# A two-layer conv and pooling trunk: the two-chunk FFN part starts at tile 6 instead of 8, a down group moves ahead of layer 1, and the second chunk's pooling mixer goes to VectorE in two halves

## Chip, core and metric

The kernel runs on one core of a Trainium2 chip. The metric is the device time of one execution in microseconds (us). Engines are named as the profile names them: PE is TensorE (matrix products), DVE is VectorE, ACT is ScalarE, POOL is GpSimd, SP is SyncE, which issues most of the transfers.

## What is computed

Two residual layers over a sequence of 1024 positions with 1024 channels, all in float32. Layer 0 mixes tokens by a causal convolution module, layer 1 by a causal multi-scale pooling mixer. Each mixer is followed by a SwiGLU feed-forward network (FFN) with 2816 hidden channels. Each part is normalised, shifted and scaled from a conditioning vector `c`, and gated back into the stream. The pooling mixer and the FFN are what the change touches:

```python
def multiscale_pool(h, w_grp, ls):          # POOL_WINDOWS = (2, 4, 8, 16)
    ...
    for gi, w in enumerate(POOL_WINDOWS):
        lo = jnp.maximum(t + 1 - w, 0)
        win_sum = cs[:, t + 1, gi] - cs[:, lo, gi]
        cnt = (t + 1 - lo).astype(jnp.float32)
        pooled.append(win_sum / cnt[None, :, None])
    pooled = jnp.stack(pooled, axis=2)
    mixed = (pooled - hf).astype(h.dtype)
    y = jnp.einsum("bsgc,gcd->bsgd", mixed, w_grp).reshape(B, S, D)
    return y * ls

def swiglu_ffn(h, w_gate, w_up, w_down):
    return (jax.nn.silu(h @ w_gate) * (h @ w_up)) @ w_down

for i in range(DEPTH):
    ...
    h = modulate(rms_norm(x, norm_mix_g[i]), sh_m, sc_m)
    y = conformer_conv(...) if i % N_MIXERS == 0 else multiscale_pool(...)
    x = x + (1.0 + g_m)[:, None, :] * y
    h = modulate(rms_norm(x, norm_ffn_g[i]), sh_f, sc_f)
    x = x + (1.0 + g_f)[:, None, :] * swiglu_ffn(h, ...)
return rms_norm(x, final_g)
```

## The kernel before

**Layout.** Channels lie on the 128 partitions, in eight tiles; positions lie along the free dimension, in two chunks A and B of 512. A float32 operand of a product is split in two parts that TensorE can take, a high part (`hi`, made by a cast, mostly on ACT) and a low part (`lo`, the rest, a subtraction, mostly on DVE). One product of tiles is three TensorE products, hi by hi, hi by lo and lo by hi (`products`, L459).

**The FFN, tile by tile.** The 2816 hidden channels are 22 tiles. A plain tile of one chunk (`ffn_p1`, L987) takes eight products of tiles for the gate and eight for the up half, 48 TensorE products in two groups of 24. `gated` (L1000) then makes silu of the gate times up, and its `hi` (ACT) and `lo` (DVE or POOL, whichever a running estimate finds free, `either`, L163). Two tiles together go through a down group (`ffn_p2`, L1044): eight outputs of six products, 48 in all, each output followed by `update` (L981) on DVE, which adds it to the stream x. The weights of plain tiles are loaded as they are, cast on ACT into a high and a negated copy, and POOL's queue adds the original to the negated one by an accumulating transfer (`load_weight`, L443); weights marked `own` get their low part from DVE instead.

**Winograd pairs.** Chunk B's FFN runs mostly in pairs of tiles by a Winograd scheme with seven block products instead of eight (`ffn_pair`, L1223): blocks over two hidden tiles, two halves of the channels and two halves of the 512 positions, so its products have 256 columns. A pair is a gate unit and an up unit of 84 products each, with down products of the pair before put among them (`Downs`, L1183). The blocks of h that the scheme wants are made once by `combined` (L1081).

**Layer 1.** It has three parts, set by `WHOLE = 8` (L62):

- tiles 0 to 7 of chunk A, plain (L1954 to L1979), while chunk B's statistics, pooling mixer, pool output and FFN norm are made beside them on the other engines;
- tiles 8 to 21 of both chunks at once, the two-chunk part (`ffn_joint`, L1572): Winograd pairs whose position halves are the chunks A and B, so products have 512 columns. A pair is two `joint_unit`s (L1479) of seven blocks of 12 products each (named `w11`, `w12`, `s2`, `s1`, `s3`, `s4`, `w22` by the part of the weights that they read). 48 down products of the pair before stand in each unit at fixed places (`GATE_SLOTS`, `UP_SLOTS`). The first unit instead holds tiles 6 and 7's down products of chunk A, after its first two blocks;
- tiles 0 to 7 of chunk B: two plain ones and three Winograd pairs, and the ending with the final norm. Chunk A's final norm (`final`, L1655) runs beside them.

**The rows of the two-chunk part.** `joint_rows` (L1422) makes the blocks of h for the two-chunk part: for each of four rows k it scales two tiles of x (`scaled`), stores one in memory (`front`), subtracts, and splits the results into the pairs `t2`, `t1`, `t3` and `t4`, eleven operations on DVE and seven on ACT. `t1` and `t4` are stored in memory and read back by every unit (`streamed`, L1469); the stored `front` tiles are read back in the last unit and split there into `hi` and `lo` for chunk B (L1516 to L1522). The rows need the norm of B's stream after its pool output, and `wholes` (L1413), sums of A's `hi` and `lo`.

**The pooling mixer.** `pool_h` (L920) scales x into eight tiles `hp`; `pool_mixed` (L940) makes the trailing sums by adds of shifted tiles (one for window 2 up to four for window 16, on DVE or POOL by `either`), subtracts h, and splits the result into `mxhi` (a cast on DVE) and `mxlo`. `pool_out` (L966) multiplies by the group weights in two halves of 24 products, adds to x and sums squares for the next norm.

**Order.** The order of TensorE's work is the order of a list of units (`unit`, L597, run by `run_units`, L609). The other engines' work is emitted by tasks that `pace` (L199) steps between groups of products, ahead of TensorE's estimated time by at most 4 us; `need` finishes a task before the next unit. A scheduler then orders each of those engines' queues by priority: urgent and eager tasks at their place, other tasks 300 places later (`LATER`), the preparation of pair weights 120 places later (`PREPARED`). Each engine runs its queue strictly in that order.

At the end of layer 0, chunk B has four plain tiles left (18 to 21; `ffn_mixed`, L1316). L1347 exchanges two units so that the down group of tiles 18 and 19 comes ahead of tile 21. A's pool output comes in front of that down group (`OUT_AT = 5`), and A's FFN norm is made under the down group and tile 21. The last down group (tiles 20 and 21) comes only after A's tile 0 of layer 1, as `joint_pend` (L1954), so chunk B's stream is complete, and its statistics and pooling start (L1969, L1970), behind that. B's pool output stands five units from the end of A's plain part (L1971).

## Time and profile before

| what | value |
|---|---|
| median of three runs | 1789.5 us (1789.5 to 1793.23) |
| profiled execution, its own time | 1788.28 us |
| its span, first to last instruction | 1786.5 us |
| PE busy | 1756.9 us, 98% of the span |
| DVE, ACT, POOL busy | 1309.4, 943.2, 518.1 us |
| transfers | 351 MB, 196 GB/s over the span |
| mean granted TensorE clock | 0.994 |

The profile comes from one execution; its times are in us from the span's start. A row of the chain or of the timeline begins with its start and its length. In a group, `out<-in` are the program's names, and the count follows an x. L118 is a helper that issues every operation of DVE, ACT and POOL, and L141 the one for products, so groups are told apart by their tiles' names: `gate` and `up` are FFN outputs, `dn` down outputs, `y` pool outputs, `w` weight parts, `t` a temporary.

### The profile page before, as it was taken

The page shows a single profiled execution, that of the slowest core. Times are in us where ns is not written, and L with a number is a line of the kernel's source. Part 1 is how long each engine was busy: PE and PEld are TensorE (multiplying, and loading weights), DVE is VectorE, ACT ScalarE, POOL GpSimd, SP SyncE. Part 2 cuts the span into 40 slices and gives each one's busy share as a digit, 9 for nine tenths or more (in the row PEclk, how much of TensorE's full clock was granted, in tenths as well). Part 3 has the DMA queues.
Part 4 walks back from the last instruction along what each step waited for, and adds up shares of the span by engine and source line. Part 5 has one row for each costly group of instructions (what it writes and reads, how often), then busy time and mean ns, then how long its engine had stood idle before and what let it go on. Part 6 is the DMA issues. An engine that isn't in the chain of part 4 may idle for free.

```text
span 1786.5 us, 24555 instructions
## 1 busy us (share of the span) xinstructions
PE 1756.9 (98%) x8930; PEld 1475.3 (83%) x8930; DVE 1309.4 (73%) x2095; ACT 943.2 (53%) x1447; POOL 518.1 (29%) x554
## 2 busy tenths in 40 slices
PE   9999999999999999999999999999999999999997
PEld 7777777888888888899999888878888888878997
DVE  8689846898775328989986877887666666657885
ACT  4766675877656455565555356464323233334553
POOL 0389722997734121211112613411000000000012
PEclk9999999999999999999999999999999999999999
DMA  9969666898978988877765577775655555566652
GB/s 306 288 178 263 172 156 175 225 234 207 241 200 205 240 216 198 223 209 203 210 198 139 126 180 168 182 204 199 226 190 191 184 207 188 188 208 166 164 144 59
DMA packets 132139, 351.03 MB, mean 196 GB/s; under 512 B 13361, under 2 KB 23729, under 8 KB 132018
## 3 DMA queue, kind: packets, MB, share of 16 engines
q1 hardware_dynamic: 104656, 263.46, 43.3%
q0 software_dynamic: 26208, 84.95, 26.7%
q8 instruction: 70, 1.15, 0.3%
q10 hardware_dynamic: 1154, 1.05, 0.2%
q14 instruction: 51, 0.42, 0.1%
HBM read 339.97 MB, written 9.44 MB: 196 GB/s over the span
## 4 chain that ended last, share of the span: by engine, by line
PE 87%; DVE 5%; issue 3%; DMA 2%; ACT 2%; POOL 1%; SPq 0%; DVEq 0%; POOLq 0%; ACTq 0%
PE dn L141 24%; PE gate L141 23%; PE up L141 23%; PE y L141 5%; PE a L141 3%; PE g L141 2%; PE first L141 2%; DVE x L118 1%; ACT w L118 1%; DVE t L118 1%; PE ada L141 1%; PE var L141 1%; ACT t L118 1%; PE idle L141 1%; DMA adaw<-in_adan_dram 1%
## 5 line engine op out<-in xcount | busy, mean ns | idle before, releaser
L118 ACT CAST w<-raw 128x512 fp32r<-128x512 f32 (+1 forms) x338 | 276.6, 822 | 162.0 <-PE gate L141 52.7
L118 DVE SCALAR_TENSOR_TENSOR x<-dn,gains,x 128x512 f32<-128x512 f32 (+1 forms) x360 | 260.9, 735 | 102.6 <-PE dn L141 97.8
L141 PE MATMUL dn<-ghi,w 128*128 128x512 f32 (+1 forms) x960 | 307.1, 387 | 3.9 <-ACT ghi L118 3.4
L141 PE MATMUL up<-hhi,w 128*128 128x512 f32 (+1 forms) x968 | 294.5, 372 | 0.0
L141 PE MATMUL gate<-hhi,w 128*128 128x512 f32 (+1 forms) x968 | 293.7, 372 | 0.6 <-ACT hhi L118 0.6
L118 ACT ACTIVATE w<-raw 128x1024 fp32r<-128x1024 f32 (+1 forms) x182 | 175.5, 964 | 184.7 <-PE up L141 55.1
L118 POOL TENSOR_TENSOR pa<-pa,pr 128x512 f32<-128x512 f32 x176 | 252.3, 1576 | 18.3 <-ACT pr L118 15.5
L453 POOL DMA_DIRECT2D w<-in_wgu_dram x76 | 68.6, 906 | 624.6 <-ACT w L118 605.1
L141 PEld LDWEIGHTS dn<-ghi,w 128*128 128x128 f32 x960 | 179.8, 190 | 38.7 <-ACT ghi L118 3.8
L141 PEld LDWEIGHTS gate<-hhi,w 128*128 128x128 f32 x968 | 177.8, 188 | 33.7 <-ACT hhi L118 0.8
L141 PEld LDWEIGHTS up<-hhi,w 128*128 128x128 f32 x968 | 177.9, 188 | 31.7
L141 PE MATMUL dn<-glo,w 128*128 128x512 f32 (+1 forms) x480 | 185.5, 387 | 1.2 <-POOL glo L118 1.1
L141 PE MATMUL dn<-gpair,w 128*128 128x512 f32 x720 | 180.0, 390 | 2.1 <-ACT w L118 1.7
L141 PE MATMUL gate<-hlo,w 128*128 128x512 f32 (+1 forms) x484 | 180.0, 372 | 0.3 <-DVE hlo L118 0.3
L141 PE MATMUL up<-hlo,w 128*128 128x512 f32 (+1 forms) x484 | 179.8, 372 | 0.0
L118 DVE SCALAR_TENSOR_TENSOR ca<-u,vecs,ca 128x512 f32<-128x512 f32 x244 | 170.5, 748 | 1.0
L141 PEld LDWEIGHTS dn<-gpair,w 128*128 128x128 f32 x720 | 134.9, 188 | 31.3 <-ACT w L118 2.1
L118 DVE TENSOR_TENSOR w<-raw,w 128x512 fp32r<-128x512 f32 (+1 forms) x156 | 121.7, 786 | 27.7 <-ACT w L118 26.6
L118 ACT ACTIVATE pr<-u,vecs 128x512 f32<-128x512 f32 x176 | 120.0, 717 | 29.0 <-POOL pa L118 21.3
L118 DVE TENSOR_TENSOR t<-t,up 128x512 f32<-128x512 f32 (+1 forms) x79 | 51.4, 651 | 93.9 <-PE up L141 93.0
L1174 POOL DMA_DIRECT2D w<-in_wgu_dram x40 | 34.8, 877 | 255.6 <-ACT w L118 89.2
L141 PEld LDWEIGHTS dn<-glo,w 128*128 128x128 f32 x480 | 91.2, 190 | 17.2 <-POOL glo L118 2.0
(253 smaller groups left out, 3292.5 us busy)
## 6 DMA issues: line engine op xcount, KB each, us to landing
raw<-in_wgu_dram SPq DMA_DIRECT2D x148, 512.0 KB, 5.4
t<-t SPq DMA_DIRECT2D x224, 256.0 KB, 4.9
w<-in_wgu_dram POOLq DMA_DIRECT2D x76, 512.0 KB, 8.1
raw<-in_wdn_dram SPq DMA_DIRECT2D x74, 512.0 KB, 5.7
adaw<-in_ada_dram SPq DMA_DIRECT2D x64, 512.0 KB, 5.2
raw<-in_w_dram SPq DMA_DIRECT2D x42, 512.0 KB, 6.5
w<-in_wdn_dram POOLq DMA_DIRECT2D x34, 512.0 KB, 8.4
adaw<-in_adan_dram SPq DMA_DIRECT2D x32, 512.0 KB, 6.6
```

What stands on the lines that cost most here:

```text
L118: self.last = self.order(getattr(self.eng, name)(out, *args, **kw))
L141: last_mm[0] = nc.tensor.matmul(out, lhsT, rhs, start=start, stop=stop, **kw).ins.name
L453: order(nc.gpsimd.dma_start(as_src(lo), src, accum_op=ADD))
L1174: order(nc.gpsimd.dma_start(lo, src, accum_op=ADD))
```

## The change

Layer 1's two-chunk part starts at tile 6, so tiles 6 and 7 leave A's plain part and B's pairs and become one more two-chunk pair. In layer 0 the exchange of units is gone: tiles 20 and 21 are followed by A's pool output, the down group of 18 and 19 and that of 20 and 21, and then layer 1 starts. B's statistics and pooling start before A's tile 0. The mixer is made in halves: the first half's pool output comes after A's tile 3, the second half's after tile 4. Its adds are all on DVE for chunk B, its high casts on ACT. In A's plain tiles the low part of `gated` is always on DVE, and for tiles 4 and 5 the gating has a priority 300 places ahead. In the last two-chunk unit the splitting of the `front` tiles stands behind the block `s4`; their transfers stay where they were. `T2_AT` and `T3_AT` say only in which half of a buffer a row's parts lie.

```diff
-WHOLE = 8
+WHOLE = 6
-T2_AT, T3_AT = ((0, 1), (0, 1), (1, 0), (0, 1)), ((1, 0), (0, 1), (0, 1), (1, 0))
+T2_AT, T3_AT = ((1, 0), (0, 1), (1, 0), (0, 1)), ((0, 1), (1, 0), (1, 0), (1, 0))
-OUT_AT = 5
+OUT_AT = 6
...
+    def pool_rows(ch, l, rstd, ks):
+        n, hp = ch.n, st["hp", ch.i]
+        for k in ks:
...
             V_.scalar_tensor_tensor(t, x[ch.i][k], scale_m[:, lk : lk + 1], rstd, op0=MUL, op1=MUL)
             S_.activation(hp[k][:, PHALO : PHALO + n], t, AF.Identity, bias=shift(l, 0, k))
...
     def pool_mixed(ch, k):
-            either(n).tensor_tensor(nxt[:, first:end], cur[:, first:end], cur[:, first - have : end - have], op=ADD)
+            (V_ if ch.i else either(n)).tensor_tensor(nxt[:, first:end], cur[:, first:end], cur[:, first - have : end - have], op=ADD)
...
-        V_.tensor_copy(hi, cur[:, PHALO:end])
+        if ch.i:
+            S_.copy(hi, cur[:, PHALO:end])
+        else:
+            V_.tensor_copy(hi, cur[:, PHALO:end])
...
-    def ffn_p1(ch, l, f, pick, soon=False, home=None):
+    def ffn_p1(ch, l, f, pick, soon=False, home=None, first=0):
...
-            gated(ch, f, outs, soon, home=home)
+            with tc.high_priority(offset=first):
+                gated(ch, f, outs, soon, home=home)
...
-        rest[-3:-1] = rest[-2], rest[-3]
...
             if last:
                 front = []
                 for src in st["kept", "front"]:
                     t = slot(A, "front", F32)
                     sync.dma_start(t, src)
-                    hi, lo = slot(A, "hhi"), slot(A, "hlo")
-                    S_.copy(hi, t)
-                    V_.tensor_tensor(lo, t, f32(hi), op=SUB)
-                    front.append((hi, lo))
+                    front.append(t)
...
             block(right, "s4", hb[half:], False)
             V_.tensor_tensor(rb, rb, right, op=ADD)
+            if last:
+                for k, t in enumerate(front):
+                    hi, lo = front[k] = slot(A, "hhi"), slot(A, "hlo")
+                    S_.copy(hi, t)
+                    V_.tensor_tensor(lo, t, f32(hi), op=SUB)
             block(a, "w22", t4, False)
...
-    pooled(rest[:-1], A, OUT_AT)
+    pooled(rest, A, OUT_AT)
...
-    def pool_whole(ch):
+    def pool_first(ch):
...
         while ("rstd", ch.i) not in st:
             yield "wait"
+        for k in range(KT // 2):
+            yield from pool_rows(ch, 1, st["rstd", ch.i], [k])
+        for k in range(KT // 2):
+            yield from pool_mixed(ch, k)
+        T["pool", 2] = Task(pool_second(ch), False, 0)
+        T["pool", 2].eager = True
+
+    def pool_second(ch):
+        yield from pool_rows(ch, 1, st.pop(("rstd", ch.i)), range(KT // 2, KT))
+        for k in range(KT // 2, KT):
+            yield from pool_mixed(ch, k)
         T["wholes"] = Task(wholes(), False, 0)
         T["wholes"].eager = True
...
-    us, joint_pend = [], rest[-1]
+    us = []
     for f in range(0, WHOLE, 2):
         home = True if f + 2 == WHOLE else None
-        us += [ffn_p1(A, 1, f, True, home=home), joint_pend, ffn_p1(A, 1, f + 1, True, home=home)]
+        p1 = lambda f: ffn_p1(A, 1, f, True, True, home, LATER if f + 3 > WHOLE else 0)
+        us += [p1(f), joint_pend, p1(f + 1)] if f else [p1(f), p1(f + 1)]
         joint_pend = ffn_p2(A, 1, [f, f + 1], True)
...
+    put(("stats", 1), lambda: stats_whole(B), True, delay=DELAY_AMONG)
+    put_eager(("pool", 1), lambda: pool_first(B))
     for i, u in enumerate(us):
         add([u])
-        if i == 1:
-            put(("stats", 1), lambda: stats_whole(B), True, delay=DELAY_AMONG)
-            put_eager(("pool", 1), lambda: pool_whole(B))
-        if i == len(us) - 5:
+        if i == len(us) - 4:
             need(("pool", 1))
             squares = Squares(B)
-            for q in range(2):
-                pool_out(B, 1, q, squares)
+            pool_out(B, 1, 0, squares)
+        if i == len(us) - 3:
+            need(("pool", 2))
+            pool_out(B, 1, 1, squares)
             put(("nf", 1), lambda: mixed_norm(squares), True, delay=DELAY_AMONG)
             put_eager("rows", joint_rows)
```

More of the change, by code (lines that the diff above doesn't have):

```diff
@@ L927, in pool_h @@
                 G_.tensor_copy(hp[k][:, :PHALO], phalo[:, k, :])
-        n = ch.n
         rstd = yield from st.pop(("spread", ch.i))
-        for k in range(KT):
+        yield from pool_rows(ch, l, rstd, range(KT))
+    def pool_rows(ch, l, rstd, ks):
+        n, hp = ch.n, st["hp", ch.i]
+        for k in ks:
             lk = l * KT + k
@@ L936, in pool_h @@
         if ch.i == 0:
-            for k in range(KT):
+            for k in ks:
                 G_.tensor_copy(phalo[:, k, :], hp[k][:, ch.n : ch.n + PHALO])
@@ L1937, in stats_whole @@
         st["rstd", ch.i] = yield from mean_rsqrt(acc, ch.n, True, "col2")
-    def given(key):
-        return st.pop(key)
-        yield
-    def pool_whole(ch):
+    def pool_first(ch):
+        hp = st["hp", ch.i] = [wslot(ch, "hp") for _ in range(KT)]
+        for k in range(KT):
+            G_.tensor_copy(hp[k][:, :PHALO], phalo[:, k, :])
         while ("rstd", ch.i) not in st:
             yield "wait"
-        st["spread", ch.i] = given(("rstd", ch.i))
-        yield from pool(ch)
+        for k in range(KT // 2):
[8 more added lines that the diff above has]
+            yield from pool_mixed(ch, k)
         T["wholes"] = Task(wholes(), False, 0)
```

## The prediction

> **What bounds the kernel now.** I read the page first: how much of the span TensorE is busy, and who holds the chain that ended last.
>
> ```profile
> span 1786.5 us, 24555 instructions
> PE 87%; DVE 5%; issue 3%; DMA 2%; ACT 2%; POOL 1%; SPq 0%; DVEq 0%; POOLq 0%; ACTq 0%
> ```
>
> TensorE products are 87% of the chain, so time comes off in two ways only: fewer product columns, or less waiting in front of products. The chain in order of time gives the price of a product near the end of the program.
>
> ```profile
> 1642.30 5.44 PE gate L141 x24
> 1647.74 5.44 PE up L141 x24
> 1653.18 10.88 PE dn L141 x48
> 1664.06 9.99 PE gate L141 x84
> ```
>
> 24 products with 512 columns take 5.44 us (0.227 each), a down group of 48 takes 10.88, and the 84 half-width products of one second-chunk pair unit 9.99 (0.119 each: half the columns for 52% of the time). Then the engine table by stretches, for whole stages:
>
> ```profile
> 1318.95:1378.80 59.85, 59.85 (x266) 49.56 (x265) 37.19 (x57) 18.45 (x33) 0.00 (x0) 1.00 0.58 194
> 1094.40:1143.90 49.50, 49.50 (x220) 40.81 (x219) 46.57 (x60) 22.32 (x28) 26.97 (x23) 1.00 0.66 155
> 1034.00:1060.90 26.90, 26.81 (x127) 22.18 (x126) 23.22 (x43) 13.99 (x19) 3.70 (x7) 1.00 0.68 172
> 1170.50:1215.00 44.50, 40.07 (x164) 32.30 (x164) 43.19 (x68) 28.14 (x48) 8.27 (x5) 0.92 0.68 201
> ```
>
> Columns: stretch, length, then busy time of PE, PEld, DVE, ACT, POOL with instruction counts, granted clock, DMA share, GB/s. The first row is one pair of the two-chunk part in its steady state: TensorE busy all 59.85 us, DVE 37.2, so a further pair there costs its products and nothing else. The last row, just ahead of the two-chunk part, is another matter: DVE busy 43.2 of 44.5 us, TensorE only 40.1. The same table for TensorE alone, around its gaps:
>
> ```profile
> 1179.80:1198.30 18.50, 14.07 (x49) 0.82 0.81 243
> 1184.30:1191.13 6.83, 5.76 (x14) 0.50 0.95 273
> 1214.65:1226.25 11.60, 11.13 (x49) 1.00 0.40 137
> 1588.20:1620.30 32.10, 30.43 (x133) 1.00 0.90 272
> 1528.40:1558.25 29.85, 29.85 (x133) 1.00 0.53 187
> ```
>
> The down group of tiles 4 and 5 takes 18.5 us in place of 10.88: 7.6 lost. Part of that is no idle time: for 6.83 us the granted clock was 0.50, which costs up to 3.4. The down group of tiles 6 and 7 at 1214.65 takes 11.6: 0.7 lost. The last unit of the two-chunk part takes 32.1 us where its twin one pair earlier takes 29.85: 2.2 lost. The waits of TensorE in these stretches, and the chain there, name the causes:
>
> ```profile
> PE dn L141 <- ACT ghi L118: 3.4, 1, 3.4
> PE dn L141 <- POOL glo L118: 1.1, 1, 1.1
> PE dn L141 <- POOL gpair L118: 0.5, 1, 0.5
> PE dn L141 <- ACT w L118: 1.7, 1, 1.7
> 1172.06 6.12 DMA front<-t
> 1594.63 8.69 DMA front<-front
> 1603.34 0.62 ACT hhi L118
> ```
>
> The gate result `ghi` of tile 5 stands in ACT's queue behind work on the second chunk's rows (`joint_rows`), which waits for a store of 6.12 us. In the last unit ACT's cast of a reloaded row waits 8.69 us for its transfer, and a weight cast and a bank eviction stand behind it.
>
> **The change, part by part.** What one DVE operation costs, from DVE's instructions in order of time:
>
> ```profile
> 1195.90 1.40 DVE L118 SCALAR_TENSOR_TENSOR t<-x,gains,ny 128x512 f32<-128x512 f32 x2
> 1205.28 0.68 DVE L118 TENSOR_TENSOR hlo<-t,hhi 128x512 fp32r<-128x512 f32 x1
> 1205.88 0.68 DVE L118 SCALAR_TENSOR_TENSOR whole<-t,whole 128x512 f32<-128x512 f32 x1
> ```
>
> An operation that reads x takes 0.66 from start to start (1.40 for two, less the 0.74 of the last), the others on 128x512 take 0.60.
>
> *Tiles 6 and 7 become two-chunk tiles.* Out go four groups of 24 products for chunk A (4 x 5.44 = 21.8) and two half-width units for B (2 x 9.99 = 20.0). In comes one Winograd pair: of the 264 products in 59.85 us, 168 are its own (84 a unit), 38.1 us; the other 96 are down products, 21.8, and those replace A's down group (10.88) and B's 48 down products (10.9). Net -3.7 us. DVE gets 37.2 us of work in those 59.85, which TensorE covers.
>
> *Gating of tiles 4 and 5 goes ahead of the row work, its low part on DVE.* `ghi` no longer stands behind the store, and POOL no longer makes `glo`. The 7.6 and 0.7 go: -8.3. What is late next is the row work itself, below.
>
> *Casts of the reloaded rows move past four product blocks.* The four ACT casts and four DVE subtractions leave the place in which they blocked; their DMAs keep theirs on SP's queue. -2.2. The rows are next needed by B's first tile, one block and one down slot later (18 products, 4.1 us); four ACT casts of 0.62 fit. If DVE, which gates the last pair there, is late with the low parts, up to 2.2 comes back.
>
> *The last down group of layer 0 moves ahead of layer 1, and its place behind A's pool output is taken up by it instead of tile 21.* The cover for A's norm stays two groups of 10.88 us. The third stretch above shows DVE busy 23.2 of 26.9 us under that cover; the moved group brings eight updates of x (0.66 each, 5.3 us) and takes away two gating operations: +4.0 against 3.7 us of idle time. I take 0.7 for this and for B's first statistics, which start on the same updates; bounds 0 (updates may lag, banks allowing) and 3. Its weight loads are SP transfers without POOL's accumulating DMA, before and after.
>
> *B's pooling mixer on DVE.* Groups of DVE and POOL during that stage (count, busy, mean ns):
>
> ```profile
> L118 DVE SCALAR_TENSOR_TENSOR t<-x,gains,ny 128x512 f32<-128x512 f32 x8 | 8.4, 1097 | 1.2 <-ACT ny L118 1.2
> L118 DVE TENSOR_TENSOR whole<-hhi,hlo 128x512 f32<-128x512 f32 x8 | 7.1, 899 | 0.0
> L118 DVE CAST mxhi<-win 128x512 fp32r<-128x512 f32 x8 | 5.7, 709 | 0.1
> L118 POOL TENSOR_TENSOR win<-hp 128x512 f32<-128x512 f32 (+3 forms) x8 | 10.5, 1312 | 5.4 <-ACT hp L118 3.8 <-DVE mxlo L118 1.6
> L118 POOL TENSOR_TENSOR win<-win 128x512 f32<-128x512 f32 (+2 forms) x7 | 8.7, 1244 | 7.2 <-DVE win L118 6.0 <-DVE mxlo L118 1.1
> ```
>
> POOL's 15 adds become DVE adds at 0.60: +9.0. The eight high casts go to ACT (8 x 0.62 = 5.0 more on an engine busy 22.3 of 49.5 us): -5.7. And `t<-x` and `whole`, 1097 and 899 ns beside POOL, take 0.74 and 0.68 without it: -2.9 and -1.8. DVE's sum gets no larger, and POOL's accumulating weight transfers no longer queue behind adds. The first half is due five groups and the second six and a half after chunk B is complete, against six for the whole before: no wait on TensorE, cost 0. If the cover failed, one add costs 0.6.
>
> *The rows get less time.* This is what the change turns on. Between B's pool output and the two-chunk part there were four groups; now there are two. DVE in order of time, and TensorE's second statistics group:
>
> ```profile
> 1032.68 0.75 DVE L118 SCALAR_TENSOR_TENSOR x<-y,gains,x 128x512 f32<-128x512 f32 x1
> 1044.96 2.74 DVE L118 SCALAR_TENSOR_TENSOR t<-x,gains,ny 128x512 f32<-128x512 f32 x4 [0.76 <-ACT ny L118]
> 1170.53 2.08 DVE L118 SCALAR_TENSOR_TENSOR t<-x,gains,ny 128x512 f32<-128x512 f32 x3 [5.46 <-ACT ny L118]
> 1214.31 0.68 DVE L118 TENSOR_TENSOR t2lo<-t,t2hi 128x512 fp32r<-128x512 f32 x1
> 1168.04 1.05 PE L141 MATMUL rstd<-ident,col 128*128 128x128 f32 x8
> ```
>
> The first scaled row follows the last pool update by 12.3 us where a down group comes behind it, as it will (1032.68 to 1044.96); I take 12.5 after the end of the pool products. TensorE needs the fourth `t2` pair after: a down group and a tile (21.8), two small statistics groups (0.9 each), two blocks (5.4), tiles 4 and 5's down products (10.9) and nine products of the block (2.0): 42.0. On DVE by then stand 40 row operations (eleven a row, seven of the fourth; eight of the 40 on x), eight updates of x, and nine others (two of gating, five weight parts, the low part of the sum `s2`, one bank add): 16 x 0.66 + 41 x 0.60 = 35.2. So the fourth pair is there 47.7 after the pool products: TensorE idles 5.7 us. Before, the same 40 among other work took 44.5 us (1170.53 to the end of 1214.31). The bounds are 0.4, if the eight updates wait behind the rows, and 15.0, if DVE mixes in as much other work as it did before. I take 5.7, from the operations that must come first.
>
> The half clock followed an idle time of 3.4 and 1.1 us, and none followed the 1.7 at 1603. At 5.7 I count it: +3.4; with a gap below about 3 it is 0. The Trainium skill (TensorE: Matmul & The Clock Gate, "What's actually happening") says that the gate looks at free-running windows of about 3.4 us, so a gap of 5.7 holds a whole one in most alignments but not in all; by the alignments that miss it the sum below would be 3.4 lower. The 6.83 us at 0.50 agree with two such windows.
>
> The last block reads `t4` back from memory. The page's list of DMA issues, with KB and median us to landing:
>
> ```profile
> t<-t SPq DMA_DIRECT2D x224, 256.0 KB, 4.9
> ```
>
> There and back is about 2 x 4.9 us. With four more DVE operations the last part lands 12.2 us behind the fourth `t2`; TensorE gets there after 10.9, or 14.3 with the half clock. 0, at most 1.3.
>
> **Sum.** -3.7 -8.3 -2.2 +0.7 +5.7 +3.4 = -4.4 us. The profiled execution took 1788.28 us (span 1786.5): 1783.9. The median of the runs is 1789.5, 1.2 above it: 1785.1.
>
> **Rivals.** *The rows are hidden after all.* The eight updates wait, the gap is 0.4, the clock stays at full: 1788.28 - 14.2 + 0.7 + 0.4 = 1775.2, 1776.4 on the median's scale. For it: eight banks let TensorE run some updates ahead. Against: the unit's code emits those updates ahead of the last rows, and the rows hold DVE's queue to the end either way.
>
> *Slower: the row stage on DVE becomes the wait.* Place: the block `s2` of the first two-chunk unit. If the row work takes the 44.5 us it took before, the gap is 12.5 + 44.5 - 42.0 = 15.0, plus 3.4 and 0.7: 1793.2, 1794.4 on the median's scale. The gain is used up at a gap of 10.1; at 13.7 the change is measurably slower. For it: DVE was busy 97% there with 68 operations, and row transfers hold buffers (the 6.12 us store). Against: much of the other work was for tiles that are gone or can follow later.
>
> *One removal doesn't work.* The reloaded rows make TensorE wait at B's first tile instead: 2.2 comes back, 1787.3, no change that can be told. For it: DVE gates the last pair at that very time. Against: ACT has 4.1 us for 2.5 of casts.
>
> **How the numbers follow.** A measurement of this kernel tells 0.2%, 3.6 us, from no change. Forecast (1781 to 1789) 0.42, of it 0.30 below 1785.9, 0.11 within, 0.01 above 1793.1. Rows hidden 0.18, all faster. Removal that fails 0.18: 0.05, 0.12, 0.01. Row stage slower 0.22: 0.03 within, 0.19 slower. Together faster 0.53, same 0.26, slower 0.21. The range 1775 to 1795 takes in both outer cases' centres and leaves their far sides out.
>
> **What would show it.** Right: no TensorE wait on `ghi` or `glo` in layer 1's first tiles; in the first two-chunk unit one gap on `t2lo` or a weight part, 3 to 10 us, with a stretch at clock 0.50 behind it; the last unit at about 29.9 us; pool adds on DVE at 0.60; eight pairs of 59.85. Wrong: a TensorE wait on `mxlo` or on A's first `hlo` above 1 us, a gap in the first unit above 13, or none at all.

## Result and profile after

The changed kernel takes 1801.4 us (median of four runs, 1800.0 to 1805.3) against 1790.7 us for the kernel before (median of four, 1789.5 to 1793.2): 1.0059 times, with a 95% interval of 1.0045 to 1.0073. Forecast was 1785.1 us, 1775 to 1795. It is slower by some 10.8 us where a gain of 4.4 was forecast. The profiled execution took 1800.02 us.

The page of the profile, and the longest waits of TensorE between chunk A's pool output and the second two-chunk unit:

```profile
span 1798.1 us, 24373 instructions
PE 89%; DVE 5%; issue 2%; ACT 1%; DMA 1%; POOL 1%; DVEq 0%; SPq 0%; POOLq 0%; ACTq 0%
```

```profile
PE dn L141 <- ACT gpair L118: 5.1, 1, 5.1
PE dn L141 <- DVE gpair L118: 2.8, 1, 2.8
PE var L141 <- DVE acc L118: 2.6, 3, 1.7
PE gate L141 <- DVE t2lo L118: 1.9, 1, 1.9
PE gate L141 <- ACT t2hi L118: 1.9, 1, 1.9
```

The waits on `ghi` and `glo` are gone, as forecast. But the same down group, tiles 4 and 5, now waits 7.9 us on `gpair`, the same values in their new place, and the block `s2` waits 3.8 more. The stretches (columns as in the prediction):

```profile
1180.00:1200.68 20.68, 12.76 (x48) 9.75 (x47) 20.68 (x35) 11.78 (x21) 0.00 (x0) 0.83 0.47 167
1185.40:1192.23 6.83, 3.85 (x8) 2.76 (x9) 6.83 (x13) 2.68 (x5) 0.00 (x0) 0.50 0.58 211
1200.68:1221.20 20.52, 16.69 (x61) 13.06 (x60) 14.26 (x23) 7.63 (x13) 0.00 (x0) 0.83 0.64 197
1205.90:1212.73 6.83, 5.52 (x13) 4.38 (x14) 4.36 (x8) 2.35 (x4) 0.00 (x0) 0.50 0.61 159
1162.72:1207.15 44.43, 32.74 (x134) 25.74 (x132) 44.42 (x73) 25.80 (x45) 0.00 (x0) 0.91 0.43 154
1629.20:1659.80 30.60, 30.50 (x133) 24.62 (x132) 14.51 (x23) 13.45 (x19) 2.62 (x3) 1.00 0.90 278
1360.00:1419.85 59.85, 59.85 (x266) 49.56 (x265) 37.26 (x57) 18.45 (x33) 0.00 (x0) 1.00 0.56 193
```

The down group, whose first product starts at 1179.62, takes 21.1 us for 10.9 of products, and `s2` with what follows 20.5 for 13.6. At each of the two places stand 6.83 us at clock 0.50. The fifth row is the row stage from the first scaled row to the end of the fourth `t2lo`: VectorE busy 44.42 of 44.43 us with 73 operations. Among them, from the groups of that stretch, are 14 low parts of pair weights:

```profile
L118 DVE TENSOR_TENSOR w<-raw,w 128x512 fp32r<-128x512 f32 x8 | 5.3, 683 | 0.0
L118 DVE TENSOR_TENSOR w<-acc,w 128x512 fp32r<-128x512 f32 x5 | 3.4, 681 | 0.0
L118 DVE TENSOR_TENSOR w<-ny,w 128x512 fp32r<-128x512 f32 x1 | 0.7, 681 | 0.0
```

The last two rows of the stretches above came out nearly as forecast: the last two-chunk unit takes 30.6 us (32.1 before, 29.9 forecast), a steady pair 59.85.

Tile 5's gating in that stage, from ScalarE's and VectorE's instructions:

```profile
1162.72 2.74 DVE L118 SCALAR_TENSOR_TENSOR t<-x,gains,ny 128x512 f32<-128x512 f32 x4 [0.16 <-ACT ny L118]
1182.02 0.58 ACT L118 ACTIVATE t<-gate 128x512 f32<-128x512 f32 x1
1184.23 0.68 DVE L118 TENSOR_TENSOR t<-t,up 128x512 f32<-128x512 f32 x1
1188.44 0.68 DVE L118 TENSOR_TENSOR gpair<-t,gpair 128x512 fp32r<-128x512 f32 x1
```

The gate products ended at 1168.7, but silu ran at 1182.0: its temporary is one of four buffers named `t`, and the first four scaled rows had taken all four at 1162.7. Two more scaled rows (at 1172.1 and 1180.6) took a buffer before silu got one.

The end of the program has a loss that the prediction does not name:

```profile
1755.53 5.39 DVE L118 SCALAR_TENSOR_TENSOR x<-x,vecs,ny 128x512 f32<-128x512 f32 x8 [0.76 <-ACT ny L118]
1760.84 1.01 DVE L118 TENSOR_TENSOR t<-t,up 128x256 f32<-128x256 f32 x2
1761.30 0.38 PE L141 MATMUL up<-thi,w 128*128 128x256 f32 x1 [2.17 <-DVE t L118]
1762.20:1765.61 3.41, 3.41 (x13) 2.92 (x12) 2.96 (x6) 1.14 (x2) 0.00 (x0) 0.50 0.14 53
```

Eight scalings of chunk A's output rows (`final`) run in one piece on VectorE ahead of the last pair's gating; TensorE waits 2.2 us and then runs 3.4 us at half clock. In the kernel before, they ran one unit earlier and in two pieces, and the same wait was 0.4 us:

```profile
1716.25 3.40 DVE L118 SCALAR_TENSOR_TENSOR x<-x,vecs,ny 128x512 f32<-128x512 f32 x5 [0.90 <-ACT ny L118]
1725.50 2.07 DVE L118 SCALAR_TENSOR_TENSOR x<-x,vecs,ny 128x512 f32<-128x512 f32 x3
```

TensorE's time over what its products take at the prices of the prediction, by place: row stage 8.4 us before, 17.1 after; chunk A's norm with its first tile 0.4 and 4.5; last two-chunk unit 2.2 and 0.7; last pair of chunk B 0.6 and 4.1. The products themselves take 3.5 us less. Together that is 11.3 of the 11.7 us between the two profiled executions.

### The profile page after: what moved, and what is told of

Same layout as the page of the kernel before. It is cut to its first block, busy times and chain, and to the rows that moved or that the text cites. A ratio compares the mean times of both kernels' runs of the same rounds, so it can differ in the third digit from the quotient of the medians.

```text
span 1798.1 us, 24373 instructions
## 1 busy us (share of the span) xinstructions
PE 1757.9 (98%) x8834; PEld 1471.4 (82%) x8834; DVE 1309.4 (73%) x2112; ACT 933.9 (52%) x1438; POOL 479.3 (27%) x524
## 4 chain that ended last, share of the span: by engine, by line
PE 89%; DVE 5%; issue 2%; ACT 1%; DMA 1%; POOL 1%; DVEq 0%; SPq 0%; POOLq 0%; ACTq 0%
PE dn L141 25%; PE up L141 24%; PE gate L141 24%; PE y L141 5%; PE a L141 3%; PE g L141 2%; PE first L141 2%; DVE x L118 1%; DVE t L118 1%; PE ada L141 1%; DVE acc L118 1%; ACT w L118 1%; PE rstd L141 1%; PE idle L141 1%; PE var L141 1%
## 5 line engine op out<-in xcount | busy, mean ns | idle before, releaser
L118 ACT CAST w<-raw 128x512 fp32r<-128x512 f32 (+1 forms) x332 | 270.2, 818 | 170.6 <-PE gate L141 57.4
L141 PE MATMUL dn<-ghi,w 128*128 128x512 f32 (+1 forms) x896 | 284.8, 385 | 0.6 <-ACT t L118 0.6
L118 ACT ACTIVATE w<-raw 128x1024 fp32r<-128x1024 f32 (+1 forms) x172 | 166.7, 969 | 187.9 <-PE up L141 55.2
L453 POOL DMA_DIRECT2D w<-in_wgu_dram x72 | 64.9, 906 | 701.7 <-ACT w L118 690.6
L141 PE MATMUL dn<-gpair,w 128*128 128x512 f32 x816 | 206.3, 392 | 8.0 <-ACT gpair L118 5.1
L141 PEld LDWEIGHTS dn<-ghi,w 128*128 128x128 f32 x896 | 167.3, 189 | 32.3 <-ACT t L118 1.0
L141 PEld LDWEIGHTS dn<-gpair,w 128*128 128x128 f32 x816 | 154.1, 189 | 41.7 <-ACT gpair L118 5.6
L141 PE MATMUL dn<-glo,w 128*128 128x512 f32 (+1 forms) x448 | 172.3, 385 | 0.1
L141 PEld LDWEIGHTS gate<-hlo,w 128*128 128x128 f32 x472 | 88.8, 188 | 18.1 <-DVE hlo L118 2.5
L141 PEld LDWEIGHTS up<-hlo,w 128*128 128x128 f32 x472 | 88.9, 188 | 15.8
```

What stands on the lines that cost most here:

```text
L118: self.last = self.order(getattr(self.eng, name)(out, *args, **kw))
L141: last_mm[0] = nc.tensor.matmul(out, lhsT, rhs, start=start, stop=stop, **kw).ins.name
L453: order(nc.gpsimd.dma_start(as_src(lo), src, accum_op=ADD))
```

## The experiments

Two theories. *Load*: VectorE is full in the row stage and in the norm, so each operation that stands ahead of a needed one costs its 0.6 us, whatever the buffers. *Buffers*: tile 5's gating is late only for want of a `t` buffer. The tables give the change in each place, read from the start of the same product in both traces (us; minus is shorter; e2 orders its products otherwise, so its row compares TensorE's losses). The runs were made in batches; the kernel before had a median of 1790.2 us beside e1 to e4, 1790.7 beside e5 to e8, 1791.0 beside e9 to e12, 1791.1 beside e13 to e15 and 1789.6 beside e16 and e17, and the ratios are to that. Where the norm of A shows +1.6 or +3.2, the wait there is as long as in the changed kernel and a half-clock stretch follows it (last section).

Variants of the changed kernel, against its profiled execution:

| run | median us | ratio to the kernel before, 95% interval | norm of A | down group, tiles 4 and 5 | s2 | end |
|---|---|---|---|---|---|---|
| e1 | 1803.9 | 1.0063 to 1.0093 | +3.2 | -10.2 | +11.6 | 0 |
| e2 | 1800.3 | 1.0043 to 1.0073 | -4.1 | +1.3 | -2.2 | 0 |
| e3 | 1802.3 | 1.0055 to 1.0085 | +1.6 | 0 | 0 | 0 |
| e4 | 1801.6 | 1.0046 to 1.0080 | +1.6 | 0 | 0 | 0 |
| e7 | 1793.2 | 1.0002 to 1.0021 | 0 | -4.5 | -3.3 | 0 |
| e8 | 1796.0 | 1.0023 to 1.0045 | +1.6 | -10.2 | +3.9 | 0 |
| e11 | 1801.1 | 1.0042 to 1.0070 | +1.6 | +0.1 | 0 | -3.7 |
| e12 | 1807.4 | 1.0083 to 1.0113 | +1.6 | +1.4 | -2.2 | 0 |
| e13 | 1792.3 | 0.9997 to 1.0015 | +3.2 | -3.6 | -4.6 | -3.6 |
| e14 | 1788.6 | 0.9979 to 0.9996 | -1.6 | -3.6 | -4.3 | -3.6 |

Variants of the kernel before, against its profiled execution:

| run | median us | ratio to the kernel before, 95% interval | down group, tiles 4 and 5 | from there to the block s1 | last two-chunk unit |
|---|---|---|---|---|---|
| e5 | 1788.5 | 0.9981 to 0.9999 | -1.6 | +1.2 | -1.6 |
| e6 | 1793.4 | 1.0007 to 1.0028 | +2.0 | +0.1 | +1.9 |
| e9 | 1794.3 | 1.0010 to 1.0029 | -7.6 | +11.1 | -0.1 |
| e10 | 1791.5 | 0.9990 to 1.0009 | -7.6 | +9.7 | -1.6 |
| e15 | 1792.6 | 0.9997 to 1.0014 | -7.6 | +11.0 | -1.6 |
| e16 | 1780.7 | 0.9933 to 0.9960 | -7.6 | +0.1 | -1.6 |
| e17 | 1788.6 | 0.9979 to 0.9997 | -7.6 | +8.5 | -1.6 |

**e1: own buffer for tile 5's gating.**

```diff
-        t = temp(ch.n) if held is None else temp(ch.n, "ny", 2)
+        t = wide("gt")[:, : ch.n] if home is not None else temp(ch.n) if held is None else temp(ch.n, "ny", 2)
```

> The changed kernel, with one edit: the gate's temporary in the gating of tiles 4 and 5 is taken from a buffer of its own and no longer from the four `t` buffers that the first rows hold. Theory of the buffers: tile 5's gating is late only because it waits for a row to give its buffer back; the 5.15 and 2.77 us waits of the first two-chunk down group on `gpair` and the half clock behind them go, and the later wait on `t2` grows by less: total 5 to 8 us shorter than the changed kernel (about 1792 to 1795 profiled, 1800.0 for the changed kernel). Theory of the load: VectorE is full for 44.4 us with 73 operations, the wait only moves from the down group to the block s2: the first goes, the second grows by as much, total within 3 us of the changed kernel (1797 to 1803).

```profile
PE gate L141 <- ACT t2hi L118: 8.8, 2, 6.2
PE gate L141 <- DVE t2lo L118: 4.9, 2, 3.4
```

```profile
1171.67 0.59 ACT L118 ACTIVATE gt<-gate 128x512 f32<-128x512 f32 x1
```

The buffer was what held tile 5: its silu now runs right behind its gate products, at 1171.7, and the down group lost nothing any more. But all of it came back at `s2`, 13.7 us of waits, as the theory of the load has it.

**e2: the moved down group back behind the first tiles of layer 1.**

```diff
-OUT_AT = 6
+OUT_AT = 5
+        rest[-3:-1] = rest[-2], rest[-3]
-    pooled(rest, A, OUT_AT)
+    pooled(rest[:-1], A, OUT_AT)
-    us = []
+    us, joint_pend = [], rest[-1]
...
+        if i == 1:
             put(("stats", 1), ...)
```

> The changed kernel, with the last down group of layer 0 put back to its place behind the first tiles of layer 1. Theory that the move is what made chunk A's norm late (its eight updates of x and the two weight lows stand on VectorE between the norm's operations): the loss of TensorE between A's pool output and layer 1's first tiles falls from about 6 us to under 1.5, total 4 to 5 us shorter (about 1795 to 1796 profiled). Rival, that the early gating and the early statistics of chunk B make that loss: it stays above 4 us, total within 1.5 us. A loss that moves on: chunk B's pool stage, now with a later place for its statistics, waits on TensorE for more than 2 us.

```profile
PE y L141 <- ACT mxhi L118: 3.0, 1, 3.0
PE y L141 <- DVE mxlo L118: 1.0, 1, 1.0
```

The norm's loss went, so the move made it; but chunk B's pool output then lost 6.8 us, since the first half of the mixer then has four groups behind the completion of chunk B's stream instead of five. The move is a trade: what it loses at A's norm it gains at B's pool output.

**e3 and e4: dates in the code alone.**

```diff
-            if i == 1 and beside is not None:
+            if i == 0 and beside is not None:
...
-            if following is not None:
+            if following is None:
...
+            elif not first:
                 following.prepare()
...
+            if first:
+                following.prepare()
+                st["ahead"]()
             block(a, "w22", t4, False)
```

> The changed kernel, with the scaling of chunk A's output rows begun one pair unit of chunk B earlier. Theory that its eight operations on VectorE (5.39 us) stand ahead of the last gating: TensorE's wait of 2.2 us on the last unit and the half clock behind it (3.4 us) go, total 3 to 5 us shorter (1795 to 1797 profiled). Rival, that the last unit's weights or its gating are late by themselves: the wait stays, total within 1 us. If the eight operations only hit the unit before, the same 2 us show there.

> The changed kernel, with the preparation of the second unit's weights moved, in the first two-chunk unit, from ahead of the block s3 to ahead of w22. Theory of the load: those operations (about six, 0.6 us each) stand among the 73 of VectorE's full stretch; taking them out makes the fourth `t2` pair 3 to 4 us earlier and shortens the total by 3 to 4 us, if the weights then do not come late. Theory of the buffers alone: the waits on `gpair` decide and the total does not change (within 1.5 us). If the preparation is late in its new place, the second unit's first block waits on its weights by 1 to 4 us and the total gets longer.

Neither changed the order of VectorE's queue in the stage that it aimed at, so they say nothing on the theories (in e4 VectorE's order is the same from end to end). When the code emits an operation hardly mattered here. The later runs tie operations by explicit dependencies or move them to another engine.

**e5: the late casts alone, on the kernel before.**

```diff
-                    hi, lo = slot(A, "hhi"), slot(A, "hlo")
-                    S_.copy(hi, t)
-                    V_.tensor_tensor(lo, t, f32(hi), op=SUB)
-                    front.append((hi, lo))
+                    front.append(t)
...
             block(right, "s4", hb[half:], False)
             V_.tensor_tensor(rb, rb, right, op=ADD)
+            if last:
+                for k, t in enumerate(front):
+                    hi, lo = front[k] = slot(A, "hhi"), slot(A, "hlo")
...
```

> The kernel before, with one part of the change alone: the casts and subtractions of the reloaded rows behind the block s4 in the last two-chunk unit. By the prediction's third term TensorE's 2.2 us there go and the total is 1.6 to 2.2 us shorter (1786 to 1787 profiled, 1788.3 before); rival: the casts now make chunk B's first tile wait and nothing is gained.

Measured 1.6 in its place, 2.2 in the median; no wait took their place in the last unit or in chunk B's first tile. The profiled execution itself is level with the one before (1788.16 and 1788.28 us): 1.2 us came at the next down group and 1.1 in the ending. The 1.6 at tiles 4 and 5 is a half-clock stretch of 3.41 us in place of 6.83, in a stage that this edit does not touch.

**e6 and e9: the early gating alone, on the kernel before.** e6 gives tiles 6 and 7 the priority, low parts on VectorE and an own temporary; e9 instead tile 5 alone, with its gated values in the `wide` buffer.

```diff
+        p1 = lambda f: ffn_p1(A, 1, f, True, f + 3 > WHOLE, home, LATER if f + 3 > WHOLE else 0)
...
+        due = f == WHOLE - 4
+        us += [ffn_p1(A, 1, f, True, home=home), joint_pend,
+               ffn_p1(A, 1, f + 1, True, due, "wide" if due else home, LATER if due else 0)]
```

> The kernel before, all eight first tiles kept, with one part of the change alone: the gating of tiles 6 and 7 (the pair ahead of the two-chunk part) goes ahead of the row work with its low parts on VectorE, its temporary in a buffer of its own. By the prediction's second term the down group that took 18.5 us takes 10.9 and the total is 7 to 8 us shorter. Theory of the load: the row stage of this kernel is as full on VectorE (43 of 44.5 us), so a part comes back as a wait on `t2lo` in the block s2; there TensorE arrives 21.8 us later than in the changed kernel, whose wait with the own buffer is 18.5 us, so at most 3 us come back: 4 to 8 us shorter. If nothing is gained, the gating was not what TensorE waited for.

> The kernel before with its eight first tiles, and one thing alone: tile 5's gating is given buffers of its own for its products and goes ahead of the row work, its low part on VectorE. (The run with eight tiles before this one moved tiles 6 and 7, but the `ghi` that TensorE waits for is tile 5's.) By the prediction's second term the down group of tiles 4 and 5 takes 10.9 in place of 18.5 us and the total is 7 to 8 us shorter. Theory of the load: with eight tiles TensorE reaches the block s2 some 19 us after the fourth `t2lo`, so nothing comes back there: the same 7 to 8 us. Rival: the wait only moves (to `t2lo`, or to the rows' transfers), less than 3 us gained; then no early gating gains anything while the row stage is full.

e6 was aimed at the wrong pair: its waits on tile 5's `ghi` and `glo` stayed (3.9 and 3.1 us). In e9 the 7.6 us went in full, and 11.0 came back in the next down group, on tile 7's gating:

```profile
PE dn L141 <- POOL gpair L118: 4.5, 1, 4.5
PE dn L141 <- ACT gpair L118: 4.3, 1, 4.3
1214.29 5.23 POOL L118 TENSOR_TENSOR gpair<-t,gpair 128x512 fp32r<-128x512 f32 x1 [26.23 <-ACT gpair L118]
```

My slack of 19 us at `s2` was right and did not matter; the down group before it was due first.

**e7 and e8: 16 weight operations behind the rows.** Only the later parts of the first unit's weights and the second unit's are moved; e8 adds e1's buffer.

```diff
+        def behind(self):
+            if self.f == WHOLE and "t2last" in st:
+                tc.add_manual_dep(V_.last.ins, st["t2last"], edge, reason="behind the rows")
...
+                finish(T["rows"])
+                wt.rest()
```

> The changed kernel, with 16 weight operations of the first two units (sums and low parts that the blocks after s2 and the second unit need) put behind the fourth `t2lo` on VectorE by explicit order; nothing else moved. This makes the list of the prediction (57 operations) true. Theory of the load: the fourth `t2lo` ends 9 to 10 us earlier after the first row (35 us in place of 44.4), the wait in s2 goes, and with it its half clock (about 7 us); the wait of the first down group on `gpair` stays or gets shorter by a few us: total 5 to 9 us shorter than the changed kernel (1791 to 1795 profiled). If the weights then come late, blocks s1 to w22 of the first unit or the second unit wait, and part of it comes back. Theory of the buffers: the 10 us loss in front of the down group stays whole, the rest changes by less than 3.

> The changed kernel, with the same order of the weights and the gate's temporary of tiles 4 and 5 in a buffer of its own. Both theories together: no wait in front of the first down group, and in s2 the 18.5 us that the own buffer alone gave, less 16 operations of 0.60: 9 us; total 8 to 10 us shorter than the changed kernel (1790 to 1792 profiled), as long as the kernel before. If the half clock is not met, 3.4 less.

```profile
1164.83:1202.15 37.32, 32.65 (x134) 25.72 (x132) 37.28 (x61) 21.77 (x38) 0.00 (x0) 0.95 0.43 155
PE dn L141 <- ACT gpair L118: 1.9, 1, 1.9
PE dn L141 <- DVE gpair L118: 1.6, 1, 1.6
PE gate L141 <- DVE t2lo L118: 0.7, 1, 0.7
```

VectorE reaches the end of the fourth `t2lo` with 61 operations in 37.3 us instead of 73 in 44.4 (twelve of the 16 had stood in that stretch), and TensorE gets 7.8 us back; twelve operations of 0.60 are 7.2. With the list of the prediction nearly true (57, 35.2 us), the stage loses 9.3 us, where the prediction had 5.7 + 3.4 = 9.1. The agreement is in the sum alone: 3.5 us of the waits stand at `gpair` and 1.3 at `t2`, where the prediction had 5.7 at `t2`. In e8 the buffer again mostly moves the wait: none at the down group, 6.5 us at `s2`. Its profiled execution is 4.0 us shorter than the changed kernel's, not the 8 to 10 expected, and e7 without the buffer is shorter still. So the size of the loss in this stage is VectorE's load in the scheduler's order, and the buffer decides where it shows.

**e10: e9 with the late casts.**

> The same with the reloaded rows' casts behind s4 too: both parts of the change that remove a wait, without its two other tiles moved. If they add up: 9 to 10 us shorter than the kernel before, about 1779 profiled; the best of all kernels here. If the first gives nothing: 2 us.

The two do not add up: the early gating again gave nothing in sum, the casts gained their 1.5, and the median is level with the kernel before.

**e11: six of the eight final scalings on GpSimd.**

```diff
+            if k < 2:
                 V_.scalar_tensor_tensor(xs, xs, V("final_g", k), rstd, op0=MUL, op1=MUL)
+            else:
+                S_.activation(xs, xs, AF.Copy, scale=V("final_g", k))
+                G_.tensor_tensor(xs, xs, rstd, op=MUL)
```

> The changed kernel, with six of the eight scalings of chunk A's output rows on GpSimd (behind a scaling on ScalarE) and two left on VectorE. Theory that the bunch of eight (5.39 us) stands ahead of the last pair's gating: TensorE's 2.4 us on `up` near 1757 go, and the half clock that follows; 3 to 4 us shorter than the changed kernel (1796 to 1797 profiled). Rival, that the gating is late by itself: no change within 1 us. If GpSimd's work slows the last unit's VectorE operations, up to 2 us longer.

3.7 us went in that place, the wait and the half clock. The total does not show it: this execution lost 1.6 us more in the norm, 1.0 in the two-chunk part and 1.1 in the ending, and the median is only 0.4 us shorter. e13 and e14 repeat the 3.6 in the same place.

**e12: the mixer as before.**

```diff
-            (V_ if ch.i else either(n)).tensor_tensor(nxt[...], ...)
+            either(n).tensor_tensor(nxt[...], ...)
-        if ch.i:
-            S_.copy(hi, cur[:, PHALO:end])
-        else:
-            V_.tensor_copy(hi, cur[:, PHALO:end])
+        V_.tensor_copy(hi, cur[:, PHALO:end])
```

> The changed kernel, with chunk B's mixer as it was before: its adds on whichever of VectorE and GpSimd is free, its high casts on VectorE. By the prediction's term of 0 for this part no TensorE wait on `mxlo` appears and the total stays within 1.5 us of the changed kernel. If the mixer on VectorE was needed for the two earlier dates, TensorE waits on `mxlo` by 2 to 6 us and the total is longer by that; if it had filled VectorE at the wrong place, shorter.

```profile
PE var L141 <- DVE acc L118: 5.0, 3, 3.0
```

4.4 us more behind chunk B's pool output, on the sums for its statistics and not on `mxlo`. So the mixer on VectorE costs nothing here, as forecast, and with the mixer as before the earlier dates are missed.

**e13 and e14: the mendings together.** e13 is e7 with e11. e14 also takes `own` from the moved group (`for i in (4,)` in place of `(4, -1)`).

> The changed kernel with the two mendings that gained by themselves: the 16 weight operations behind the fourth `t2lo` (gained 7.8 us of TensorE time between the first down group's start and the second unit) and six of the eight final scalings on GpSimd (gained 3.7 us near the end). If the losses are separate places, the gains add: 11 to 12 us shorter than the changed kernel, 1787 to 1790 profiled, level with the kernel before or up to 2 us shorter. If a place hides another, less than 8.

> The same, and the weights of the down group that was moved ahead of layer 1 are made with the accumulating transfer instead of two low parts of 1.22 us on VectorE (two more casts on ScalarE). Theory that these two operations stand among the updates ahead of chunk A's norm: of the about 6 us that TensorE loses from A's pool output to layer 1's first tile about 2.4 go, 2 to 3 us shorter than the run before it here. Rival, that the eight updates and ScalarE's weight casts make that loss: no change within 1 us, or longer by the two casts.

In e13 the gains of the two places add (8.2 and 3.6), less 3.2 of half clock in the norm and 1.1 in the ending; the profiled execution is 7.2 us shorter than the changed kernel's, not the 11 to 12 expected. Its median, 1792.3, is 0.9 below e7's, so what the scalings on GpSimd are worth in the total stays open. In e14 the wait of 1.7 us on `acc` ahead of A's statistics is gone, and no half clock stands there. Of the 2.4 expected there 1.6 came; the 2.7 lost in A's first tile stay. e14's profiled execution spans 1787.7 us, 10.4 less than the changed kernel's, of a miss of 16.1. In the three mended places TensorE has 13.1 us back (7.9, 1.6 and 3.6); 2.1 were lost in the program's first 240 us, which no edit touches. The row stage now loses 9.2 us, what the terms of the forecast leave there. What remains against the forecast in the places of the change is 1.8 us at A's norm and 0.7 of the late casts. In A's first tile ScalarE is busy in every moment in the changed kernel:

```profile
1068.95:1076.57 7.62, 6.56 (x26) 4.27 (x24) 7.07 (x11) 7.62 (x13) 2.13 (x5) 1.00 0.77 176
```

**e15, e16 and e17: eight tiles, everything early.** e15 is e10 with the gating of tiles 6 and 7 early too and e7's order; e16 leaves `w11` and `w12` out of that order; e17 leaves the order out.

```diff
+            if self.f == WHOLE and "t2last" in st and (self.which or self.made):
```

> The kernel before with eight first tiles, with the reloaded rows' casts late, the gating of tiles 5, 6 and 7 ahead of the row work with low parts on VectorE, and the 16 weight operations behind the fourth `t2lo`. The run with tile 5 alone gained 7.6 us in its own down group and lost 11.0 in the next, where tile 7's gating waited for one of the four `t` buffers and for GpSimd. If taking 16 operations (9.6 us of VectorE) out of the row stage gives the buffers back early enough, the second wait falls under 3 us and the total is 6 to 10 us shorter than the kernel before (1779 to 1783 profiled). If the four buffers, held by the rows until their stores land, are what decides, the wait of 5 us or more stays in one of the two groups and the total is within 3 us of the kernel before.

> The run with eight tiles, all gating early and the weights behind the rows, but the halves w11 and w12 that the first two blocks of the first two-chunk unit read stay at their early place (there they stood behind the fourth `t2lo` too, and TensorE waited 9.5 us for one of them). If that wait was the edit's own, it goes and nothing takes its place: 9 to 12 us shorter than that run, about 1778 to 1781 profiled, 8 to 10 us shorter than the kernel before and the fastest here. If the row stage's load decides, a wait on `t2lo` of 5 us or more takes its place and the total stays within 3 us of the kernel before.

> The same with the weight operations back where the kernel before has them: early gating of tiles 5 to 7 and the late casts alone. Theory that the gating waits for `t` buffers which the rows give back late because VectorE is full: a wait of 4 us or more on `gpair` returns in one of the two down groups, total 4 to 10 us longer than the run beside it. If the early gating alone is enough, the two runs are within 2 us.

```profile
PE gate L141 <- DVE w L118: 9.5, 1, 9.5
```

```profile
PE up L141 <- DMA t<-t: 0.7, 1, 0.7
PE dn L141 <- DVE gpair L118: 0.5, 1, 0.5
1170.50:1215.00 44.50, 43.99 (x195) 36.08 (x194) 43.22 (x70) 27.89 (x48) 2.11 (x3) 1.00 0.68 202
```

```profile
PE dn L141 <- DVE gpair L118: 3.1, 1, 3.1
PE dn L141 <- ACT gpair L118: 3.1, 1, 3.1
```

e15 is level with the kernel before instead of 6 to 10 us shorter; its wait was the edit's own, since it goes in e16. e16 is the fastest kernel here: 1780.7 us, 0.9947 times the kernel before (0.9933 to 0.9960). VectorE is as busy as ever in the row stage (43.2 of 44.5 us, 70 operations), but what TensorE needs stands ahead of what it does not, and TensorE is busy 44.0 us there, 40.1 before. e17 shows that the early gating alone loses 8.5 again.

## Why the prediction was wrong

- *Products, -3.7*: right (-3.5).
- *Late casts, -2.2*: right in kind; -1.6 alone (e5), -1.5 in the changed kernel.
- *Mixer on VectorE, 0*: right; its alternative costs 4.4 here (e12).
- *First scaled row 12.5 us behind the pool products*: right (13.0).
- *"The 7.6 and 0.7 go: -8.3"*: failed. The waits on `ghi` and `glo` went, but I read only which queue tile 5's gating stood in and not which buffer it needs. In the new order it waits for a `t` buffer, and the down group loses 10.2 us. Even where tile 5 goes first, as much comes back elsewhere: at `s2` in e1, in the next down group in e9.
- *"I take 5.7, from the operations that must come first"*: the step that failed. I counted 57 operations by what TensorE needs; VectorE runs a queue in the order of a scheduler, and 73 stood there, among them 14 low parts of weights and four sums (a fifth begins as the stretch ends) where I had counted six weight operations in all. The time, 44.4 us, is the 44.5 that the prediction had quoted from before and set aside. TensorE's waits were 11.8 us in sum instead of 5.7. With the operations nearly in the order that I assumed (e7) the stage's loss is right within 0.2 us, in part by luck, since its waits stand in other places. This step and the one above are about half of the miss (7.9 of 16.1 us).
- *Half clock, +3.4*: one stretch forecast, two met, each 6.83 us long; beside the waits they cost 5.3 us in sum. The stage as a whole lost 8.7 us more than before, where the terms gave 0.8.
- *Moved down group, +0.7 (bounds 0 to 3)*: mis-sized; 4.1 measured. The eight updates were counted, but not the two low parts of 1.22 us among them (e14), nor A's first tile, where 2.7 us are lost and ScalarE is full.
- *The end*: +3.5 with no term at all. With one pair less behind chunk A's end, A's final scaling falls on the last unit; the prediction moved two tiles and did not follow what ran beside them.
- Of the rivals, "the row stage on DVE becomes the wait" named the cause and its 44.5 us. In the row stage it gave 15.0 + 3.4 = 18.4 us lost, and 17.1 were. Its 1793.2 is 6.8 short, since it lacked the norm and the end (3.4 and 3.5).
- Of the signs of being wrong none appeared: no wait on `mxlo`, 0.6 us on A's first `hlo`, and 11.8 us of waits in the first unit, below 13. They did not watch the down group's new buffer, the norm's statistics or the end.

What stays open: that tile 7 in e9 and e17 waits for one of the four `t` buffers is read from the order of the queues; a fifth buffer was not tried. Nor did a run take ScalarE's weight casts out of A's first tile, so what bounds that tile is not shown. And no run has the order of the weights alone on the kernel before.

## What to carry over

When a change takes cover away from a stage whose helper engine is full, count what that engine's queue will hold in its real order, not what the next product needs; the old stage's own duration is the better estimate. Ask of each step moved ahead which buffer it takes and who holds it, and of each work that shrinks what ran beside its end. A saturated queue can still be harmless: with the gating of tiles 5 to 7 early, the casts late and the unneeded weight operations tied behind the needed ones (e16), the kernel before gains 9 us without moving any tile, and 8 of them go when the tie goes (e17).

## What the runs showed of the hardware

The same wait can cost three amounts. In nine profiled executions, of the changed kernel and eight variants, TensorE waited 1.71 us for `acc` ahead of A's statistics and then had about 1 us of one-column products; the products behind them lost 0 us in two, 1.6 in five and 3.2 in two. The same stretch of time in the changed kernel and in e13:

```profile
1050.00:1060.00 10.00, 10.00 (x51) 8.46 (x51) 7.32 (x20) 3.12 (x4) 2.59 (x5) 1.00 0.06 14
1050.00:1060.00 10.00, 10.00 (x37) 8.30 (x37) 4.62 (x16) 0.00 (x0) 0.00 (x0) 0.66 0.01 2
```

TensorE is busy throughout in both, with 51 products and with 37: the clock is 1.00 in the one and 0.66 in the other. In e14, where that wait is gone, no half clock follows. The prediction had set the half clock at 0 for gaps below about 3 us; a gap of 1.71 with such products behind it is enough in seven of nine. The Trainium skill (TensorE: Matmul & The Clock Gate, "What's actually happening") says that the gate's windows run freely, so that the same code meets them in another phase each time; these runs agree, but the page's condition of a whole idle window of about 3.4 us is not needed here.

GpSimd beside a busy VectorE was slow here, or made it slow. The low part of `gpair` on GpSimd took 5.23 us in e9 (2.18 for the same form at 1185.9), while VectorE's operations beside it kept their 0.68; and in e11, beside the scalings on GpSimd, a VectorE low part of the last pair took 1.41 us in place of 0.69:

```profile
1759.53 1.41 DVE L118 TENSOR_TENSOR w<-raw,w 128x512 fp32r<-128x512 f32 x1
```

The Trainium skill (SBUF — State Buffer, "Who interferes with whom") says that a VectorE instruction with two inputs in this memory contends with a GpSimd instruction that reads it; the two durations agree, though no run here isolates that cause.
